# A diffusion transformer layer: when up's seeds are copied, which memory the first modulated tokens take, and where the second token tile's transposes stand

## The chip, the cores and the metric

The kernel runs on one core of a Trainium2 chip. The metric is the device time of one execution in microseconds, the median of several runs. A core has a matrix engine (TensorE, PE in the profile, with its weight loads as PEld), a vector engine (VectorE, DVE), a scalar engine (ScalarE, ACT), GpSimd (POOL) and SyncE (SP), which issues most transfers. Each engine works through its own instructions in the order in which they were written out; between engines there are only semaphores. Matrix results go to eight banks of accumulation memory (PSUM), each 128 x 512 numbers; everything else lies in the core's main memory (SBUF), where a buffer that is given to a new use must first be done with the old one.

## The reference

One layer over 256 latent tokens of width 2048 and 256 context tokens. The conditioning vector gives shifts, scales and gates; the tokens are modulated, attended and projected, normalised, modulated again and sent through a gated feed-forward block of hidden width 5632, and normalised once more. What matters here is the middle of this:

```python
sh1, sc1, g1, sh2, sc2, g2 = ada_mods(c, w_ada[layer], b_ada[layer])
...
x = layer_norm(DN_ALPHA * x + g1 * (heads @ w_out[layer]), ln1_g[layer], ln1_b[layer])
x = layer_norm(DN_ALPHA * x + g2 * swiglu(modulate(x, sh2, sc2), w_gate[layer], w_up[layer], w_down[layer]),
               ln2_g[layer], ln2_b[layer])
```

with `modulate(x, shift, scale) = x * (1 + scale) + shift` and `swiglu(u) = (silu(u @ w_gate) * (u @ w_up)) @ w_down`.

## The kernel before

**Products.** Float32 products are made of three passes: a number is split into a high part that the matrix engine takes (`hi`, an ACT cast, L330) and a remainder (`lo`, a DVE subtraction, L331), and `mm3` adds hi·hi (L340), lo·hi (L341) and hi·lo (L342). The tokens are split likewise into `u2h` and `u2l`. A loaded piece of weights is 512 columns by two groups of 128 rows; it serves both token tiles (t = 0, 1; 128 tokens each), so that one piece carries twelve passes of 512 columns.

**The transition into the feed-forward block.** The first token tile is normalised, and its columns 0 to 3 (groups of 128) are transposed by `z_flip(0, kk)` (L1444) into two banks. Meanwhile PE forms the conditioning vector's sums (`m1_sums`, L1413; PE multiplies the loaded conditioning weights there). `z_rest(t, kk)` modulates two columns with ACT (L1651), casts them into `u2h` (L1653) and DVE subtracts the remainder into `u2l` (L1654). Its working tile `uf2` comes from the pool `pb`, tag `t2k`, which begins where the earlier phase's buffers lay. `first_products(i, t, js)` then multiplies these columns by the first pieces of w_gate (i = 0) and w_up (i = 1). For the second tile, `scalars(1)` (a chain of small DVE instructions that ends with L1227, the normalised columns), `z_flip(1, kk)`, `second_shifts` (small matmuls L1426, DVE L1429) and `z_rest(1, kk)` follow. The conditioning sums of DVE (L465) are put between by the tile scheduler, which orders the instructions after this region by their data; up to the region's end (`region.__exit__`) the order is that of the code. A later `z_part(kk)` does the same as `z_flip` and `z_rest` for both tiles at once (L1471, L1476, L1478, L1479).

**The feed-forward block.** Ten of the eleven blocks of 512 hidden columns are done in five pairs f0 = 0, 2, 4, 6, 8. In a pair, `folded` forms one quarter of w_gate's contraction with seven products in place of eight: sums and differences of weight pieces (DVE L1535, L1538, L1539, L1545, L1547) and ACT copies from bank to bank (L1534, L1542, L1550) stand between the products. Between these, `up` multiplies the pieces of w_up into two banks of the `wk` pool. From the second pair on these banks start from an earlier partial sum kept in main memory (`spill`): ACT copies it into the banks (L1724, the seeds), and after the last piece ACT copies the sum back (L1730); in the first pair DVE adds (L1732). Then the gate's remaining pieces follow, and `gated_half` adds gate's earlier part (DVE L1558) and takes Silu (ACT L1559). DVE multiplies by up (L1599), and the result is turned by a DVE transposition (L1569) and a trip through DRAM (SP, L1574 and L1579). At a pair's start the code of the next pair begins only after the Silu of the last gate.

**Small things.** `grp`, a table for a later reduction of the conditioning vector, is formed by DVE at its first use (L1149), and `onesr` by an ACT cast (L1767) whose place the scheduler picks.

Of the kernel before, what the change touches and what calls it, by code (L numbers as in the profile page):

```python
# [265 lines left out]
def dit_layer(ctx: ExitStack, tc: tile.TileContext, x, c, cx, c_ctx, w_ada, b_ada, w_in, q_norm_g,  # L266
# [876 lines left out]
    grp = []  # L1143

    def folded_columns(sb, n):

        if not grp:
            grp.append(pb.tile([P, 32], F32, tag="grp", name="grp"))
            nc.vector.reduce_sum(grp[0], ident.rearrange("p (a i) -> p i a", a=4), axis=AX.X)  # L1149
        r = pb.tile([P, 32], F32, tag="fold", name="fold")  # L1150
        for h in range(0, n, 4):
            t = pb.tile([P, NB], F32, tag="t2k", name="flip", bufs=4)
            nc.vector.transpose(t, sb[:, h * P : (h + 4) * P])
            nc.vector.reduce_sum(r[:, 4 * h : 4 * h + 16], t.rearrange("p (b r) -> p b r", r=32), axis=AX.X)
# [307 lines left out]
    u2h = pb.tile([P, KD, SEQ], F32R, tag="u2h", name="u2h")  # L1462
    u2l = pb.tile([P, KD, SEQ], F32R, tag="u2l", name="u2l")
    hTh = [pb.tile([P, 4, SEQ], F32R, tag=f"hTh{f}", name="hTh") if f < KF // 4 - SPLIT_F else None for f in range(KF // 4)]
    hTl = [pb.tile([P, 4, SEQ], F32R, tag=f"hTl{f}", name="hTl") if f < KF // 4 - SPLIT_F else None for f in range(KF // 4)]
# [179 lines left out]
    def z_rest(t, kk):  # L1645

        ps = zbanks[t, kk]
        tt = slice(t * P, (t + 1) * P)
        uf = pb.tile([P, 2, SEQ], F32, tag="t2k", name="uf2", bufs=4)[:, :, :P]
        for j in range(2):  # L1650
# [52 lines left out]
    def turn():  # L1703
# [3 lines left out]
        for e in [e for e in flips if e[0] <= 0]:  # L1707
            flips.remove(e)
            e[1]()

    for f0 in range(0, SPLIT_F, 2):
        for f in (f0, f0 + 1):
            if 5 <= f < 9:
                residual_base(f - 5)
        ups = {}

        def up(i, g):
            f = f0 + i
            su = [spills[f][1][:, t, :] for t in range(NT)]
            if g == groups[f]:  # L1720
                ups[i] = [wk_bank() for _ in range(NT)]
                for t in range(NT):
                    if f0:
                        nc.scalar.copy(ups[i][t], su[t])  # L1724
            project(ups[i], w_up, f, g, groups[f] * 4, KD - 1, f0 > 0)
            turn()
            if g == ng - 1:
                for t in range(NT):
                    if f0:
                        nc.scalar.copy(su[t], ups[i][t])  # L1730
                    else:
                        nc.vector.tensor_add(su[t], su[t], ups[i][t])  # L1732

# [31 lines left out]
    g2sb = pb.tile([P, D], F32, tag="u2h", name="g2sb")  # L1765
    onesr = pb.tile([P, P], F32R, tag="onesr", name="onesr")
    nc.scalar.copy(onesr, ones)  # L1767
    def l2_loads():
# [151 lines left out]
```

## Time and profile before

| what | value |
|---|---|
| runs of the kernel | 1128.13, 1130.04, 1130.06 us; median 1130.04 us |
| the profiled execution | 1130.85 us, of which the span of the instructions is 1129.1 us |
| mean granted clock of the matrix engine in it | 0.996 of full speed |
| DVE busy | 880.7 us, 78% of the span, 1105 instructions |
| ACT busy | 589.1 us, 52% of the span, 859 instructions |
| data read from and written to DRAM | 304.07 MB and 16.25 MB |

The profile is read from the outside in: the share of busy time says which engine can be the bound, the waits say what that engine stood still for, and the timeline around such a wait says which instruction came last there. In a timeline row stand the start and the duration in us, the engine, the line and operation, what is written from what, how many instructions the row joins, and in brackets how long the engine had stood idle before and what ended that.

### The profile page before, as it was taken

To read this page: it belongs to the slowest core of one execution; us is meant where nothing else is said; L and a number is where in the kernel's file an instruction comes from. 1 tells how busy PE (TensorE), PEld (TensorE's weight loads), DVE (VectorE), ACT (ScalarE), POOL (GpSimd) and SP (SyncE) were. 2 spreads that over 40 slices of the span, in tenths; PEclk is the share of its full clock that TensorE was granted. 3 is DMA by queue.
4 is the path that set the end of the run, shared out by engine and by line. 5 is a ranking of instruction groups with operands and counts; after the bars stand their busy time and mean duration, and the time that the engine had idled before them with its cause. 6 is when DMAs were issued, how large, how long until landed. Compare 5 with 4: busy or idle time off the path is not lost.

```text
span 1129.1 us, 14104 instructions
## 1 busy us (share of the span) xinstructions
PE 1104.7 (98%) x5225; PEld 884.8 (78%) x5225; DVE 880.7 (78%) x1105; ACT 589.1 (52%) x859; POOL 35.1 (3%) x82
## 2 busy tenths in 40 slices
PE   8999999999999999999999999999999999999996
PEld 6766688777887687888888878888788888888884
DVE  5763589899999798777778786988976788676576
ACT  3341554878685255444465565766754344343442
POOL 1000030110100000000000000000000000000000
PEclk9999999999999999999999999999999999999998
DMA  9999999778999769898956767778788798887542
GB/s 322 390 382 375 389 362 372 248 237 282 342 325 386 254 260 312 302 349 310 335 174 219 249 194 254 235 246 265 225 273 276 274 373 297 305 318 259 191 147 75
DMA packets 178318, 321.26 MB, mean 285 GB/s; under 512 B 8733, under 2 KB 43197, under 8 KB 175944
## 3 DMA queue, kind: packets, MB, share of 16 engines
q1 hardware_dynamic: 177528, 320.03, 81.1%
q8 instruction: 41, 0.67, 0.2%
q10 hardware_dynamic: 720, 0.33, 0.1%
q14 instruction: 29, 0.23, 0.1%
HBM read 304.07 MB, written 16.25 MB: 284 GB/s over the span
## 4 chain that ended last, share of the span: by engine, by line
PE 86%; DMA 6%; DVE 3%; ACT 3%; SPq 1%; issue 1%; ACTq 0%; DVEq 0%
PE acc L340 22%; PE acc L342 22%; PE acc L341 22%; PE wk L340 5%; PE wk L342 5%; PE wk L341 5%; DMA raw<-in_w_in_dram 3%; PE wk L1080 2%; PE wk L653 1%; DVE lo L331 1%; DMA raw<-in_w_out_dram 1%; DMA lgb<-in_ln_g_dram 1%; DMA spill<-hd 1%; DMA pd<-hx 1%; SPq L568 1%
## 5 line engine op out<-in xcount | busy, mean ns | idle before, releaser
L330 ACT CAST hi<-raw 128x1024 fp32r<-128x1024 f32 x273 | 284.7, 1054 | 272.2 <-PE acc L342 212.3
L331 DVE TENSOR_TENSOR lo<-raw,hi 128x1024 fp32r<-128x1024 f32 x273 | 328.9, 1219 | 117.6 <-ACT hi L330 113.4
L340 PE MATMUL acc<-hi,u2h 128*128 128x512 f32 x422 | 165.0, 391 | 2.0 <-ACT u2h L1653 1.5
L341 PE MATMUL acc<-lo,u2h 128*128 128x512 f32 x422 | 164.3, 389 | 0.0
L342 PE MATMUL acc<-hi,u2l 128*128 128x512 f32 x422 | 164.1, 390 | 0.0
L602 ACT CAST hi<-raw 128x1024 fp32r<-128x1024 f32 (+1 forms) x86 | 87.4, 1030 | 116.1 <-DMA raw<-in_w_in_dram 64.2
L465 DVE SCALAR_TENSOR_TENSOR adav<-raw,cs,adav 128x512 f32<-128x512 f32 (+1 forms) x128 | 121.2, 947 | 19.2 <-DMA raw<-in_w_ada_dram 17.2
L340 PE MATMUL acc<-hi,hTh 128*128 128x512 f32 x344 | 133.5, 389 | 0.4 <-ACT acc L1845 0.4
L342 PE MATMUL acc<-hi,hTl 128*128 128x512 f32 x344 | 133.7, 389 | 0.0
L341 PE MATMUL acc<-lo,hTh 128*128 128x512 f32 x344 | 133.7, 389 | 0.0
L605 DVE TENSOR_TENSOR lo<-raw,hi 128x1024 fp32r<-128x1024 f32 (+1 forms) x86 | 101.3, 1194 | 16.9 <-ACT hi L602 16.4
L340 PE MATMUL acc<-hi,uh 128*128 128x512 f32 x256 | 103.8, 405 | 1.7 <-ACT uh L768 0.8
L341 PE MATMUL acc<-lo,uh 128*128 128x512 f32 x256 | 100.6, 393 | 0.6 <-DVE lo L605 0.5
L342 PE MATMUL acc<-hi,ul 128*128 128x512 f32 x256 | 100.1, 391 | 0.4 <-DVE ul L783 0.4
L340 PEld LDWEIGHTS acc<-hi,u2h 128*128 128x128 f32 x422 | 79.1, 188 | 19.4 <-ACT u2h L1653 2.4
L340 PE MATMUL wk<-hi,u2h 128*128 128x512 f32 x232 | 90.5, 390 | 2.9 <-ACT wk L1724 2.9
L342 PEld LDWEIGHTS acc<-hi,u2l 128*128 128x128 f32 x422 | 79.2, 188 | 17.3 <-DVE u2l L1654 0.6
L341 PEld LDWEIGHTS acc<-lo,u2h 128*128 128x128 f32 x422 | 79.2, 188 | 16.2
L342 PE MATMUL wk<-hi,u2l 128*128 128x512 f32 x232 | 90.3, 389 | 0.0
L341 PE MATMUL wk<-lo,u2h 128*128 128x512 f32 x232 | 90.3, 389 | 0.0
L340 PEld LDWEIGHTS acc<-hi,hTh 128*128 128x128 f32 x344 | 64.6, 188 | 14.1 <-ACT acc L1845 0.8
L342 PEld LDWEIGHTS acc<-hi,hTl 128*128 128x128 f32 x344 | 64.6, 188 | 13.5
(262 smaller groups left out, 1552.3 us busy)
## 6 DMA issues: line engine op xcount, KB each, us to landing
raw<-in_w_ada_dram SPq DMA_DIRECT2D x70, 1024.0 KB, 7.9
raw<-in_w_gate_dram SPq DMA_DIRECT2D x44, 1024.0 KB, 6.5
raw<-in_w_up_dram SPq DMA_DIRECT2D x44, 1024.0 KB, 6.3
raw<-in_w_down_dram SPq DMA_DIRECT2D x44, 1024.0 KB, 5.3
raw<-in_w_ada_dram SPq DMA_DIRECT2D x48, 512.0 KB, 6.8
raw<-in_w_in_dram SPq DMA_DIRECT2D x18, 1024.0 KB
raw<-in_w_out_dram SPq DMA_DIRECT2D x16, 1024.0 KB, 4.9
pd<-hx SPq DMA_DIRECT2D x64, 128.0 KB, 5.0
```

What stands on the lines that cost most here:

```text
L330: nc.scalar.copy(hi[:, :n], raw[:, s : s + n])
L331: nc.vector.tensor_tensor(lo[:, :n], raw[:, s : s + n], hi[:, :n].bitcast(F32), op=ALU.subtract)
L340: nc.tensor.matmul(ps, lhsT=xh, rhs=w[0], start=first, stop=False, skip_group_check=seeded)
L341: nc.tensor.matmul(ps, lhsT=xh, rhs=w[1], start=False, stop=False, skip_group_check=seeded)
L342: nc.tensor.matmul(ps, lhsT=xl, rhs=w[0], start=False, stop=last, skip_group_check=seeded)
L465: nc.vector.scalar_tensor_tensor(a[:, c : c + piece], raw[:, f : f + piece], cs[:, 4 * (g * (G4 * NB // w) + j) + 2, None], a[:, c : c + p ...
L568: nc.sync.dma_start(room.t, w[k0 * P : (k0 + 1) * P, c0 : c0 + width])
L602: nc.scalar.copy(hl.hi[:, :n], raw.t[:, s : s + n])
L605: nc.vector.tensor_tensor(hl.lo[:, :n], raw.t[:, s : s + n], hl.hi[:, :n].bitcast(F32), op=ALU.subtract)
L653: nc.tensor.matmul(bank.t[32 * j : 32 * j + 32, :width], lhsT=cs[:, 4 * k + 2 - 2 * i : 4 * k + 34 - 2 * i], rhs=raw.t[:, c * width : (c + ...
L1080: nc.tensor.matmul(o_ps.t[:, : 2 * P].rearrange("p (g q) -> p g q", q=32), lhsT=v, rhs=pv[:, k], start=k == 0, stop=k == 3)
```

## The change

Four things are altered.

1. The four `uf2` tiles of `z_rest` are allocated at once, directly behind `u2h` and `u2l` (`rests`), so that they lie in other memory than before; what is allocated from `pb` after them moves along by 8 KB per partition.
2. `first_products(1, 0, ...)` multiplies three columns ahead of `z_flip(1, kk)` in place of two, and one after it in place of two. The copy of the conditioning sum (`adav1`) follows behind.
3. `grp` and `onesr` are formed at the region's end.
4. Up's seeds are copied by a function `seeds(f)`. `up` calls it where its block has no banks yet; for the first block of the next pair it is called ahead of the gate's last pieces and Silu of the second block of the pair before.

```diff
+    def group_sums():
+        grp.append(pb.tile([P, 32], F32, tag="grp", name="grp"))
+        nc.vector.reduce_sum(grp[0], ident.rearrange("p (a i) -> p i a", a=4), axis=AX.X)
+
     def folded_columns(sb, n):
 
-        if not grp:
-            grp.append(pb.tile([P, 32], F32, tag="grp", name="grp"))
-            nc.vector.reduce_sum(grp[0], ident.rearrange("p (a i) -> p i a", a=4), axis=AX.X)
...
+    rests = {(t, kk): pb.tile([P, 2, SEQ], F32, tag="t2k", name="uf2", bufs=4)[:, :, :P] for t in range(NT) for kk in (0, 2)}
...
-        uf = pb.tile([P, 2, SEQ], F32, tag="t2k", name="uf2", bufs=4)[:, :, :P]
+        uf = rests[t, kk]
...
     scalars(1)
+    first_products(0, 0)
+    first_products(1, 0, (0, 1, 2))
+    for kk in (0, 2):
+        z_flip(1, kk)
+    first_products(1, 0, (3,))
     adav1 = vector_sums(NB)
     nc.scalar.copy(adav1, bank1.t)
-    first_products(0, 0)
-    first_products(1, 0, (0, 1))
-    for kk in (0, 2):
-        z_flip(1, kk)
-    first_products(1, 0, (2, 3))
...
+    group_sums()
+    onesr = pb.tile([P, P], F32R, tag="onesr", name="onesr")
+    nc.scalar.copy(onesr, ones)
     region.__exit__(None, None, None)
...
+    ups = {}
+
+    def seeds(f):
+        ups[f] = [wk_bank() for _ in range(NT)]
+        for t in range(NT):
+            if f > 1:
+                nc.scalar.copy(ups[f][t], spills[f][1][:, t, :])
+
...
-        ups = {}
-
         def up(i, g):
             f = f0 + i
             su = [spills[f][1][:, t, :] for t in range(NT)]
-            if g == groups[f]:
-                ups[i] = [wk_bank() for _ in range(NT)]
-                for t in range(NT):
-                    if f0:
-                        nc.scalar.copy(ups[i][t], su[t])
-            project(ups[i], w_up, f, g, groups[f] * 4, KD - 1, f0 > 0)
+            if f not in ups:
+                seeds(f)
+            project(ups[f], w_up, f, g, groups[f] * 4, KD - 1, f0 > 0)
...
         for i, f in enumerate((f0, f0 + 1)):
+            if i and f + 1 < SPLIT_F:
+                seeds(f + 1)
             for g in range(groups[f], ng):
```

The changed code's lines stand one to eight lines lower (the seeds' copy is L1722, gate's sum and Silu L1560 and L1561). Three places show how the instructions move.

**The second token tile, ACT and DVE.** On ACT, with the semaphores waited for, the modulations of the first tile stood like this before (`uf_...` are the working tiles, `DMAHW` are transfers; the row L1767 is the cast of `onesr`):

```order
L1651 ACTIVATE uf_3724<-wk,mB,mA 128x128 [waits DMAHW2_49,DMAHW4_49,DMAHW1_49,DMAHW5_49,PE_49,Pool_49]
L1651 ACTIVATE uf_3724<-wk,mB,mA 128x128
L1767 CAST onesr<-ones 128x128 [waits DMAHW2_49,DMAHW1_49]
L1653 CAST u2h<-uf_3724 128x2x128 [waits Activation_49]
L1651 ACTIVATE uf_3729<-wk,mB,mA 128x128 x2
```

and now:

```order
L1653 ACTIVATE uf_3698<-wk,mB,mA 128x128 [waits PE_49,Pool_49]
L1653 ACTIVATE uf_3698<-wk,mB,mA 128x128
L1655 CAST u2h<-uf_3698 128x2x128 [waits Activation_49]
L1653 ACTIVATE uf_3699<-wk,mB,mA 128x128 [waits PE_49]
L1653 ACTIVATE uf_3699<-wk,mB,mA 128x128
L1655 CAST u2h<-uf_3699 128x2x128 [waits Activation_49]
```

The waits for transfers are gone, and the wait for PE is one for each of the two transposed banks: `uf_3698` no longer shares memory with the loaded conditioning weights, so that only the transposes and the modulation's coefficients (POOL) are waited for, where before the last `m1_sums` was the PE instruction that had to be over. On DVE, from the end of the second tile's `scalars(1)` on, the rows before were these (L465 are conditioning sums, L1429 `second_shifts`, L1654 the second tile's two remainders):

```order
L1227 TENSOR_SCALAR xt<-xt,mv,ly 128x512
L465 SCALAR_TENSOR_TENSOR adav<-raw,cs,adav 128x512 x3
L1429 TENSOR_TENSOR sh_147<-wk,bcol 128x8
L1654 TENSOR_TENSOR u2l<-uf_3788,u2h 128x2x128
L1654 TENSOR_TENSOR u2l<-uf_3793,u2h 128x2x128
L1227 TENSOR_SCALAR xt<-xt,mv,ly 128x512 x6
```

and now:

```order
L1228 TENSOR_SCALAR xt<-xt,mv,ly 128x512
L465 SCALAR_TENSOR_TENSOR adav<-raw,cs,adav 128x512 x2
L1430 TENSOR_TENSOR sh_147<-wk,bcol 128x8
L465 SCALAR_TENSOR_TENSOR adav<-raw,cs,adav 128x512
L1656 TENSOR_TENSOR u2l<-uf_3700,u2h 128x2x128
L465 SCALAR_TENSOR_TENSOR adav<-raw,cs,adav 128x512
L1656 TENSOR_TENSOR u2l<-uf_3701,u2h 128x2x128
```

A fourth sum has come ahead of the second remainder, and one sum now stands between the shifts and the first remainder.

**The next columns, PE.** `z_part(4)` and `z_part(6)` transpose eight squares of the normalised tokens (L1471, now L1473) in the middle of the first blocks' products. The products that read the new columns are those that wait for ACT for the second time. Before:

```order
L1471 MATMUL wk<-ident,xt 128x128 x8
L340 MATMUL acc<-hi,u2h 128x512 [waits Activation_49]
L340 MATMUL acc<-hi,u2h 128x512
L341 MATMUL acc<-lo,u2h 128x512 [waits DVE_49]
L342 MATMUL acc<-hi,u2l 128x512
L341 MATMUL acc<-lo,u2h 128x512
L340 MATMUL acc<-hi,u2h 128x512 [waits Activation_49]
```

and now:

```order
L1473 MATMUL wk<-ident,xt 128x128 x3
L340 MATMUL acc<-hi,u2h 128x512 [waits Activation_49]
L341 MATMUL acc<-lo,u2h 128x512 [waits DVE_49]
L342 MATMUL acc<-hi,u2l 128x512
L340 MATMUL acc<-hi,u2h 128x512
L341 MATMUL acc<-lo,u2h 128x512
L342 MATMUL acc<-hi,u2l 128x512
L340 MATMUL acc<-hi,u2h 128x512
L341 MATMUL acc<-lo,u2h 128x512
L342 MATMUL acc<-hi,u2l 128x512
L340 MATMUL acc<-hi,u2h 128x512
L340 MATMUL acc<-hi,u2h 128x512 [waits Activation_49]
```

Ten passes over older columns follow the transposes, where there were five. On ACT one weight cast (L330) that stood between the two casts of the new columns now stands ahead of their modulation.

**A pair's start, ACT and DVE.** On ACT the rows around the Silu of the first pair's last gate were, at the start of pair f0 = 2:

```order
L1559 ACTIVATE spill<-spill 128x512 x2
L330 CAST hi<-raw 128x1024 x3
L1724 COPY wk<-spill 128x512
L1559 ACTIVATE spill<-spill 128x512 x2
L1534 COPY acc<-wk 128x512
L1724 COPY wk<-spill 128x512
L330 CAST hi<-raw 128x1024 x4
```

and now:

```order
L1722 COPY wk<-spill 128x512
L330 CAST hi<-raw 128x1024 x5
L1561 ACT_TABLE_LOAD
L1561 ACTIVATE spill<-spill 128x512 x2
L330 CAST hi<-raw 128x1024 x4
L1561 ACTIVATE spill<-spill 128x512 x2
L1536 COPY acc<-wk 128x512
L330 CAST hi<-raw 128x1024 x3
```

Both seeds have gone up past the first Silu (the other one stands higher still), and a fourth cast stands ahead of the second. On DVE the order at the starts of pairs 4, 6 and 8 has changed with it; pair 8 before:

```order
L331 TENSOR_TENSOR lo<-raw,hi 128x1024
L1599 TENSOR_TENSOR spill<-spill 128x512
L1538 TENSOR_TENSOR raw<-raw 128x1024
L1569 STREAM_TRANSPOSE spill<-spill 128x4x4x32
L331 TENSOR_TENSOR lo<-raw,hi 128x1024 x2
L1539 TENSOR_TENSOR raw<-raw 128x1024
L331 TENSOR_TENSOR lo<-raw,hi 128x1024
```

and now:

```order
L331 TENSOR_TENSOR lo<-raw,hi 128x1024
L1601 TENSOR_TENSOR spill<-spill 128x512
L331 TENSOR_TENSOR lo<-raw,hi 128x1024
L1571 STREAM_TRANSPOSE spill<-spill 128x4x4x32
L1540 TENSOR_TENSOR raw<-raw 128x1024
L1541 TENSOR_TENSOR raw<-raw 128x1024
L331 TENSOR_TENSOR lo<-raw,hi 128x1024 x2
```

Both subtractions of `folded` (L1538 and L1539, now L1540 and L1541) now stand ahead of the remainder of up's second pair of pieces; before, one of them came behind it.

More of the change, by code (lines that the diff above doesn't have):

```diff
@@ L1729, in up @@
                     if f0:
-                        nc.scalar.copy(su[t], ups[i][t])
+                        nc.scalar.copy(su[t], ups[f][t])
                     else:
-                        nc.vector.tensor_add(su[t], su[t], ups[i][t])
+                        nc.vector.tensor_add(su[t], su[t], ups[f][t])
         def between(n):
@@ L1765, in dit_layer @@
     g2sb = pb.tile([P, D], F32, tag="u2h", name="g2sb")
-    onesr = pb.tile([P, P], F32R, tag="onesr", name="onesr")
-    nc.scalar.copy(onesr, ones)
     def l2_loads():
```

## The prediction

> **What bounds the kernel now.** First the page, for the engine that can be the bound, then the waits of that engine.
>
> ```profile
> span 1129.1 us, 14104 instructions
> PE 1104.7 (98%) x5225; PEld 884.8 (78%) x5225; DVE 880.7 (78%) x1105; ACT 589.1 (52%) x859; POOL 35.1 (3%) x82
> PE wk L340 <- ACT wk L1724: 2.9, 2, 2.3
> PE acc L340 <- ACT u2h L1653: 1.5, 1, 1.5
> PE acc L340 <- ACT u2h L1478: 0.5, 1, 0.5
> ```
>
> PE is busy for 98% of the span, so the time is PE's work, which the change leaves as it is, plus what PE stands still. The three waits (line, what ended the wait, us in total, times, longest) are those that the change reaches, 4.9 us in all; a fourth, for L1227, shows in the row of 398.31 below with 0.30. Nothing here can bring more than about that, and it is had only where the next thing PE needs is not late too. So I walk through each place in the timeline. Passes of 512 columns start 0.228 us apart, as the rows below show (394.42 to 397.62: 14 passes).
>
> **The transition.**
>
> ```profile
> 389.85 0.44 PE L1444 MATMUL wk<-ident,xt 128*128 128x128 f32 x2
> 390.22 1.92 PE L1413 MATMUL wk<-raw,cs 128*32 128x512 f32 x16
> 391.81 0.30 SPq L448 DMA_DIRECT2D adav<-in_b_ada_dram  x1
> 392.26 0.81 ACT L1651 ACTIVATE uf<-wk,mB,mA 128x128 f32<-128x128 f32 x2 [6.81 <-PE wk L1413]
> 393.14 0.41 ACT L1653 CAST u2h<-uf 128x256 fp32r<-128x256 f32 x1
> 393.61 0.50 PE L340 MATMUL acc<-hi,u2h 128*128 128x512 f32 x1 [1.47 <-ACT u2h L1653]
> 394.42 0.40 PE L340 MATMUL acc<-hi,u2h 128*128 128x512 f32 x1
> 397.62 0.39 PE L342 MATMUL acc<-hi,u2l 128*128 128x512 f32 x1
> 397.62 0.55 DVE L1227 TENSOR_SCALAR xt<-xt,mv,ly 128x512 f32<-128x512 f32 x1
> 398.08 2.32 DVE L465 SCALAR_TENSOR_TENSOR adav<-raw,cs,adav 128x512 f32<-128x512 f32 x3
> 398.31 0.63 PE L1444 MATMUL wk<-ident,xt 128*128 128x128 f32 x4 [0.30 <-DVE xt L1227]
> 398.69 0.47 PE L340 MATMUL acc<-hi,u2h 128*128 128x512 f32 x1
> 400.17 0.95 PE L1426 MATMUL wk<-sel,adav 128*128 128x4 f32 x8
> 401.15 0.17 DVE L1429 TENSOR_TENSOR sh<-wk,bcol 128x8 f32<-128x8 f32 x1 [0.76 <-PE wk L1426]
> 401.24 0.75 DVE L1654 TENSOR_TENSOR u2l<-uf,u2h 128x256 fp32r<-128x256 f32 x2
> 401.71 0.50 PE L342 MATMUL acc<-hi,u2l 128*128 128x512 f32 x1
> 404.67 1.21 DVE L331 TENSOR_TENSOR lo<-raw,hi 128x1024 fp32r<-128x1024 f32 x1
> ```
>
> ACT's first modulation waited for the last L1413, though its banks were transposed by 390.3. With other memory the two modulations (0.81) and casts (0.41) of both column pairs are over by about 391.6, while PE is still at L1413 to 392.14. PE's first product then starts at about 392.2 in place of 393.61. In the new order 21 passes follow: 392.2 + 0.34 for the first + 20 x 0.228 = 397.1. The transposes take 0.38 (398.31 to 398.69): 397.5. Their DVE chain starts about 2.5 us earlier, after the earlier remainder, and ends near 395.1, so this wait goes. Three passes (0.78, with a restart) and L1426 (0.81 to the next product) give 399.1, and the first L342 on the second tile could come 0.54 later at 399.6, where it stood at 401.71.
>
> There DVE is late next. It works two sums, then L1429, which waits for L1426 until about 399.2 and takes 0.17, a third sum (2.32/3 = 0.77) and the first remainder (0.38): 400.5. The L342 starts at 400.55: **1.16 us gained** of 2.1. The bounds: 2.1 if the sums weren't in the way; 0.7 if the sums can't start before 398.08, where they start now and where I can't see since when their data was there (two to 399.6, L1429, third sum, remainder to 400.95). I take 1.16, since the bias row that the first sum adds to (L448) was asked for at 391.81, 6.3 us before 398.08. The next need is the first gate remainder (L331, 404.67 + 1.21 = 405.88). On DVE `grp` (0.36) now stands ahead of it and the six normalisations start earlier, so it ends where it did; PE comes to it at about 405.95. That margin is nothing: up to 0.2 may go there.
>
> **The next columns.**
>
> ```profile
> 434.42 1.03 PE L1471 MATMUL wk<-ident,xt 128*128 128x128 f32 x8
> 436.22 0.40 PE L341 MATMUL acc<-lo,u2h 128*128 128x512 f32 x1
> 436.48 0.62 ACT L1478 CAST u2h<-uf 128x512 fp32r<-128x512 f32 x1
> 437.15 0.50 PE L340 MATMUL acc<-hi,u2h 128*128 128x512 f32 x1 [0.53 <-ACT u2h L1478]
> 437.45 1.05 ACT L330 CAST hi<-raw 128x1024 fp32r<-128x1024 f32 x1
> ```
>
> PE should have started a pass at 436.45 and started at 437.15: 0.70 lost. Now ten passes in place of five stand ahead of this product, so PE reaches it 1.14 later, at about 437.6. The weight cast that stood behind (1.05, less the idle time of ACT that it fills) now stands ahead of the modulation and puts the cast's end from 437.1 to about 437.5. **0.70 gained**, with a bound of 0.5 if the cast is 0.1 to 0.2 later than that.
>
> **The seeds, pair 2.**
>
> ```profile
> 651.81 1.27 DVE L1558 TENSOR_TENSOR spill<-spill,acc 128x512 f32<-128x512 f32 x2
> 652.09 0.39 PE L342 MATMUL wk<-hi,u2l 128*128 128x512 f32 x1
> 652.52 1.23 ACT L1559 ACTIVATE spill<-spill 128x512 f32<-128x512 f32 x2 [3.85 <-DVE spill L1558]
> 653.00 1.22 DVE L1538 TENSOR_TENSOR raw<-raw 128x1024 f32<-128x1024 f32 x1
> 654.17 0.58 ACT L1724 COPY wk<-spill 128x512 f32<-128x512 f32 x1
> 654.80 0.50 PE L340 MATMUL wk<-hi,u2h 128*128 128x512 f32 x1 [2.32 <-ACT wk L1724]
> ```
>
> The second seed stands behind two Silu and a bank copy, and these wait 3.85 us for DVE. The pass due at 652.32 starts at 654.80: 2.48 lost. With the seed copied long before, PE goes on. Next late could be DVE, which doesn't get faster: behind L1538 (653.00, 1.14 to the next) come L1599 (0.60) and the remainder of the third piece (1.13), ready at 655.9; PE, 24 passes after 650.96, needs it at about 656.65. Following DVE on to the pair's next remainders I find margins of 0.5 to 1.5 us everywhere, so **2.48 gained**; below, 1.7 if DVE runs 1.2 us behind this count.
>
> The Trainium skill, in "PSUM — Partial Sum Buffer", section "Engine vs sequencer instructions", says that ScalarE's queue is strictly first in, first out; the row of 654.17 agrees, since a copy whose data had long been there waited behind a Silu. By that rule a seed that is moved up takes whatever it waits for with it, which speaks against the change and is the second rival.
>
> **The seeds, pairs 4, 6 and 8.**
>
> ```profile
> 791.02 1.10 ACT L1724 COPY wk<-spill 128x512 f32<-128x512 f32 x2
> 791.65 0.50 PE L340 MATMUL wk<-hi,u2h 128*128 128x512 f32 x1 [0.56 <-ACT wk L1724]
> 792.72 0.69 DVE L1599 TENSOR_TENSOR spill<-spill 128x512 f32<-128x512 f32 x1 [0.16 <-ACT spill L1559]
> 793.33 1.22 DVE L1538 TENSOR_TENSOR raw<-raw 128x1024 f32<-128x1024 f32 x1
> 795.09 2.32 DVE L331 TENSOR_TENSOR lo<-raw,hi 128x1024 fp32r<-128x1024 f32 x2
> 797.33 1.22 DVE L1539 TENSOR_TENSOR raw<-raw 128x1024 f32<-128x1024 f32 x1
> ```
>
> Pairs 4 and 6 have no wait for a seed. At pair 8 the product due at 790.93 started at 791.65: 0.72 lost, and saved. But here the new DVE order costs: L1599 still starts near 792.7 (a weight cast on ACT takes the time of the seeds), then a remainder (1.14), the transposition (0.63), L1538 and L1539 (1.14 each) and the remainder that up's second pair of pieces needs (1.18), together with L1599's 0.61 ready at 798.5. PE, 30 passes and two more after 790.93, wants it at 798.2. A stall of 0.3 to 0.5 is new: **0.27 gained** net. The same order at pairs 4 and 6 leaves, by the same count, margins of 0.3 to 0.5 and 0.85 us: nothing gained or lost.
>
> What else moves (`grp`, `onesr`, `adav1`'s copy) is under 0.7 us on engines that wait there, and I cost it at nothing; without that cover it would be 0.3 for each cast or reduction.
>
> **The sum.** 1.16 + 0.70 + 2.48 + 0.27 = 4.6 us off the profiled execution's 1130.85, of which 1.75 lie around the span: 1126.25. That execution is 0.8 above the median of 1130.04, so the forecast on that scale is **1125.5 us**. The most, with nothing given back, is 2.1 + 0.70 + 2.48 + 0.72 = 6.0: 1124.0. The least by the bounds above is 0.7 - 0.2 + 0.5 + 1.7 + 0 = 2.7: 1127.3.
>
> **The rivals.** First: DVE takes the gain back at the pairs' starts. For it: L1538 and L1539 now stand together ahead of a remainder at three starts, and the margins are small. Against it: that DVE has idle time between the starts and begins each of them fresh. If DVE runs 1.0 us later than I count, the starts lose 0.4 at pair 2, 0.6 at pair 4, 0.15 at pair 6 and 1.0 more at pair 8: 2.2 of the 4.6, so 1127.6.
>
> Second, slower: the moved seeds hold up ACT. ACT works in order, and casts stand behind each of the eight seeds that moved. A seed waits for its bank; if it waits as long as the longest wait above, 3.85 us, the weight cast behind it is late by that less ACT's usual idle time ahead of a cast:
>
> ```profile
> 630.76 1.05 ACT L330 CAST hi<-raw 128x1024 fp32r<-128x1024 f32 x1 [1.66 <-PE acc L342]
> ```
>
> So it costs from a wait of 1.66 on, 2.2 us each. One of the two in each of four pairs would cost 8.8, and 1130.0 - 4.6 + 8.8 = 1134.2. Against it: in the new order a seed waits for a bank's copy or sum that ends where ACT now idles.
>
> Third: the seed of pair 2 doesn't come earlier after all, because its bank isn't free until the last products: then 2.48 stays, 1128.0. Against it: the order shows the copies ahead of the first Silu, and nothing of the last gate in what they wait for.
>
> **How the numbers follow.** My forecast with its own range, 1124.0 to 1126.6, has a chance of 0.60; the first rival, 1126.6 to 1128.6, 0.24; the third 0.08; the second 0.05; still faster than 1124.0, 0.03. A measurement of this kernel can tell about 0.2% or 2.3 us, so faster means under 1127.8. Faster: 0.60 + 0.03 + half of the first rival (0.13) + a little of the third (0.02) = 0.78; slower 0.05; within 0.2% the rest, 0.17. The range goes from 1123.5, half a microsecond of scatter under the most, to 1128.5, which takes in the first and the third rival.
>
> **What would show it.** Right: no wait of PE for L1653's successor above 0.1 us, the first product near 392.2, a wait for u2l or for DVE of up to 0.9 near 400, no wait for a seed at pair 2, a wait for lo near 0.4 at pair 8. Wrong: a PE wait for lo above 0.5 us at the starts of pairs 4 or 6, an ACT wait at a seed of more than 1.6 us, or a product at 394 still.

## The result, and the profile after

| what | before | changed |
|---|---|---|
| median of 7 runs each, us | 1129.85 (1126.93 to 1130.32) | 1124.39 (1123.15 to 1127.95) |
| profiled execution, us | 1130.85 | 1124.52 |
| its span, us | 1129.1 | 1122.7 |

The changed kernel takes 0.996 of the time of the kernel before, with an interval from 0.9945 to 0.9975. That is 5.5 us between the medians, with bounds of 2.8 and 6.2 us. The forecast was 1125.5, and the time lies inside its range. How much of that was insight and how much the luck of one profiled execution is what the experiments are about.

First the page of the changed kernel, and of PE's waits (line, what ended the wait, us in total, times, longest) all that end behind the transition.

```profile
span 1122.7 us, 14106 instructions
PE 1104.0 (98%) x5225; PEld 886.7 (79%) x5225; DVE 880.7 (78%) x1105; ACT 589.9 (53%) x859; POOL 36.4 (3%) x82
PE acc L342 <- DVE u2l L1656: 0.7, 1, 0.7
PE acc L340 <- ACT acc L1853: 0.4, 1, 0.4
```

PE's busy time is what it was (1104.0 beside 1104.7). Of the waits that the change reaches, the four of before are gone and one is new, for u2l; the wait for L1853 stood in the profile of before too (there it is L1845). So the whole gain is standstill taken away, and it can be added up place by place.

The transition in the changed kernel's timeline:

```profile
387.85 0.81 ACT L1653 ACTIVATE uf<-wk,mB,mA 128x128 f32<-128x128 f32 x2 [3.57 <-PE wk L1445]
389.04 1.92 PE L1414 MATMUL wk<-raw,cs 128*32 128x512 f32 x16
390.89 0.50 PE L340 MATMUL acc<-hi,u2h 128*128 128x512 f32 x1
...
395.28 1.54 DVE L465 SCALAR_TENSOR_TENSOR adav<-raw,cs,adav 128x512 f32<-128x512 f32 x2 [1.44 <-DMA adav<-in_b_ada_dram]
395.79 0.60 PE L1445 MATMUL wk<-ident,xt 128*128 128x128 f32 x4
396.93 0.95 PE L1427 MATMUL wk<-sel,adav 128*128 128x4 f32 x8
397.91 0.17 DVE L1430 TENSOR_TENSOR sh<-wk,bcol 128x8 f32<-128x8 f32 x1 [1.10 <-PE wk L1427]
398.00 0.75 DVE L465 SCALAR_TENSOR_TENSOR adav<-raw,cs,adav 128x512 f32<-128x512 f32 x1
398.66 0.42 DVE L1656 TENSOR_TENSOR u2l<-uf,u2h 128x256 fp32r<-128x256 f32 x1
399.13 0.50 PE L342 MATMUL acc<-hi,u2l 128*128 128x512 f32 x1 [0.68 <-DVE u2l L1656]
```

ACT's modulation is now released by the transposes (L1445) and runs beside L1414, so the first product stands right behind the conditioning sums, 1.85 us after the start of the last L1414 row, where it stood 3.39 us after it (390.22 to 393.61). What is late next is DVE, as forecast: its conditioning sum stands between the shifts and the remainder. Counted from the same PE row, because both executions share all code up to there, the first L342 on the second tile came after 11.49 us and comes after 10.09 (399.13 - 389.04): 1.40 us gained.

The next columns (L1473 transposes them, and the cast L1480 releases their product):

```profile
431.93 1.04 PE L1473 MATMUL wk<-ident,xt 128*128 128x128 f32 x8
432.72 0.48 PE L340 MATMUL acc<-hi,u2h 128*128 128x512 f32 x1
434.44 0.62 ACT L1480 CAST u2h<-uf 128x512 fp32r<-128x512 f32 x1
434.89 0.73 PE L340 MATMUL acc<-hi,u2h 128*128 128x512 f32 x2
```

From 432.72 to 434.89 PE runs without a gap: nine passes, 0.31 apart behind the transposes and then 0.23, and the row of two L340 at 434.89 joins the tenth and the first product on the new columns, 0.70 us gained.

The seeds: how the view of one line shows all sixteen copies (start of the first and the last, then how long ACT stood idle before one, and until when; who waited for them is an empty list):

```profile
L1722 ACT COPY wk<-spill x16: 582/591/603, 605.5 to 798.4; 128x512 f32<-128x512 f32 x16
  DVE spill L1547: 1.1, 1
who waited for it (us, times):
```

The first seed is copied at 605.5, where the first stood at 648.1 before. The one that PE waited for at pair 2 is the second; it is copied at 624.42, and PE comes to its bank at 649.11, twelve passes after the pair's first product into `wk`, as before:

```profile
624.42 0.58 ACT L1722 COPY wk<-spill 128x512 f32<-128x512 f32 x1
649.11 0.39 PE L340 MATMUL wk<-hi,u2h 128*128 128x512 f32 x1
```

PE waits for none; between these two executions 2.48 us are gained at pair 2 and 0.72 at pair 8. Pair 8's start, where the forecast expected a new stall:

```profile
782.94 1.24 ACT L336 CAST hTh<-spill 128x512 fp32r<-128x512 f32 x2 [0.57 <-DMA spill<-hd]
790.88 2.35 DVE L331 TENSOR_TENSOR lo<-raw,hi 128x1024 fp32r<-128x1024 f32 x2
791.95 0.62 PE L340 MATMUL wk<-hi,u2h 128*128 128x512 f32 x2
792.41 0.39 PE L341 MATMUL wk<-lo,u2h 128*128 128x512 f32 x1
```

The first of the two remainders is ready at about 792.06 (790.88 plus half of 2.35), and PE wants it at 792.41: a margin of 0.35 us, and no stall.

The sum in these two executions is 1.40 + 0.70 + 2.48 + 0.72 = 5.30. From the last L1414 row to the end the kernel before took 738.88 us (1129.1 - 390.22) and the changed one takes 733.66 (1122.7 - 389.04): 5.22 us. The other 1.2 us of the 6.4 between the spans lie ahead of that row, in code that the change doesn't touch: the row's start lay between 388.9 and 390.3 in all the profiles of this study, of either order. It is scatter and no part of the gain.

### The profile page after: what moved, and what is told of

The parts are those of the page before. It is cut to its first block, busy times and chain, and to the rows that moved or that the text cites. A ratio compares the mean times of both kernels' runs of the same rounds, so it can differ in the third digit from the quotient of the medians.

```text
span 1122.7 us, 14106 instructions
## 1 busy us (share of the span) xinstructions
PE 1104.0 (98%) x5225; PEld 886.7 (79%) x5225; DVE 880.7 (78%) x1105; ACT 589.9 (53%) x859; POOL 36.4 (3%) x82
## 4 chain that ended last, share of the span: by engine, by line
PE 94%; DMA 3%; ACT 1%; DVE 1%; issue 0%; ACTq 0%; SPq 0%; DVEq 0%
PE acc L340 24%; PE acc L342 23%; PE acc L341 23%; PE wk L340 6%; PE wk L342 6%; PE wk L341 5%; PE wk L1080 2%; DMA raw<-in_w_in_dram 2%; PE wk L653 2%; PE wk L754 1%; DMA xt<-in_x_dram 0%; PE wk L1414 0%; ACT hi L602 0%; PE wk L484 0%; PE wk L688 0%; PE wk L983 0%
## 5 line engine op out<-in xcount | busy, mean ns | idle before, releaser
L330 ACT CAST hi<-raw 128x1024 fp32r<-128x1024 f32 x273 | 285.8, 1055 | 279.8 <-PE acc L342 212.6
L340 PE MATMUL acc<-hi,u2h 128*128 128x512 f32 x422 | 165.0, 391 | 0.0
L342 PE MATMUL acc<-hi,u2l 128*128 128x512 f32 x422 | 164.2, 390 | 0.7 <-DVE u2l L1656 0.7
L341 PE MATMUL acc<-lo,u2h 128*128 128x512 f32 x422 | 164.3, 389 | 0.0
L340 PE MATMUL acc<-hi,hTh 128*128 128x512 f32 x344 | 133.5, 389 | 0.4 <-ACT acc L1853 0.4
L342 PE MATMUL acc<-hi,hTl 128*128 128x512 f32 x344 | 133.8, 389 | 0.0
L341 PE MATMUL acc<-lo,hTh 128*128 128x512 f32 x344 | 133.8, 389 | 0.0
L465 DVE SCALAR_TENSOR_TENSOR adav<-raw,cs,adav 128x512 f32<-128x512 f32 (+1 forms) x128 | 121.3, 947 | 13.7 <-DMA raw<-in_w_ada_dram 10.5
L340 PE MATMUL acc<-hi,uh 128*128 128x512 f32 x256 | 103.8, 405 | 2.1 <-ACT uh L768 0.8
L341 PE MATMUL acc<-lo,uh 128*128 128x512 f32 x256 | 100.5, 393 | 0.4 <-DVE lo L605 0.4
L342 PE MATMUL acc<-hi,ul 128*128 128x512 f32 x256 | 100.1, 391 | 0.4 <-DVE ul L783 0.4
L342 PEld LDWEIGHTS acc<-hi,u2l 128*128 128x128 f32 x422 | 79.2, 188 | 17.6 <-DVE u2l L1656 1.1
L340 PEld LDWEIGHTS acc<-hi,u2h 128*128 128x128 f32 x422 | 79.2, 188 | 17.3 <-ACT u2h L1655 0.8
L341 PEld LDWEIGHTS acc<-lo,u2h 128*128 128x128 f32 x422 | 79.2, 188 | 16.3
L341 PE MATMUL wk<-lo,u2h 128*128 128x512 f32 x232 | 90.3, 389 | 0.0
L342 PE MATMUL wk<-hi,u2l 128*128 128x512 f32 x232 | 90.3, 389 | 0.0
L340 PE MATMUL wk<-hi,u2h 128*128 128x512 f32 x232 | 89.8, 389 | 0.0
L340 PEld LDWEIGHTS acc<-hi,hTh 128*128 128x128 f32 x344 | 64.6, 188 | 14.3 <-ACT acc L1853 0.8
L342 PEld LDWEIGHTS acc<-hi,hTl 128*128 128x128 f32 x344 | 64.6, 188 | 13.5
```

Source lines behind the costliest of these rows:

```text
L330: nc.scalar.copy(hi[:, :n], raw[:, s : s + n])
L340: nc.tensor.matmul(ps, lhsT=xh, rhs=w[0], start=first, stop=False, skip_group_check=seeded)
L341: nc.tensor.matmul(ps, lhsT=xh, rhs=w[1], start=False, stop=False, skip_group_check=seeded)
L342: nc.tensor.matmul(ps, lhsT=xl, rhs=w[0], start=False, stop=last, skip_group_check=seeded)
L465: nc.vector.scalar_tensor_tensor(a[:, c : c + piece], raw[:, f : f + piece], cs[:, 4 * (g * (G4 * NB // w) + j) + 2, None], a[:, c : c + p ...
```

## The experiments

Each part of the change alone, and each taken away. The theory: the memory frees the transition, the later transposes free the next columns, the early seeds free pair 2, and DVE gives some back. The rivals: the memory alone does all of the transition and the rest is chance of the scheduler's order; or the seeds bring less than their stall shows, because DVE is late behind them. The first four kernels shared 29 runs of the kernel before, median 1128.96 us. The third part, `grp` and `onesr`, has no run of its own.

**The seeds alone** (part 4 on the kernel before).

```diff
+            if f not in ups:
+                seeds(f)
...
+            if i and f + 1 < SPLIT_F:
+                seeds(f + 1)
```

> The kernel before with the seeds part alone. If each wait is its own loss: the waits for L1724 (2.48 at pair 2, 0.72 at pair 8) go, the waits at 393.6, 398.3, 401.7 and 437.2 stay; 3.2 us faster than the kernel before, some 1126.6 us. If the seeds only pay because the transition starts the feed-forward block earlier, or if the vector engine takes the gain back at the pairs' starts: under 1.5 us faster, with waits for lo (L331) in their place.

Measured: 1127.04 us, a ratio of 0.9982 (0.9972 to 0.9991): 1.9 us, with bounds of 1.0 and 3.2. The waits of the transition and the next columns stay as before (1.47, 0.33, 0.53), no seed is waited for, and a wait for a remainder is new at pair 8. (Two more are small: PE loses 0.12 us at 656.43, in pair 2, and 0.09 at 671.64 to remainders that end 0.05 earlier.) From this kernel's timeline at pair 8:

```profile
783.14 1.05 ACT L330 CAST hi<-raw 128x1024 fp32r<-128x1024 f32 x1 [2.91 <-DMA raw<-in_w_up_dram]
784.76 1.29 DVE L1599 TENSOR_TENSOR spill<-spill 128x512 f32<-128x512 f32 x2 [0.93 <-ACT spill L1559]
795.22 2.36 DVE L331 TENSOR_TENSOR lo<-raw,hi 128x1024 fp32r<-128x1024 f32 x2
795.31 0.61 PE L340 MATMUL wk<-hi,u2h 128*128 128x512 f32 x2
796.50 0.50 PE L341 MATMUL wk<-lo,u2h 128*128 128x512 f32 x1 [0.57 <-DVE lo L331]
```

This is the stall that the prediction put there: two passes after 795.31, 0.46 later, PE wants the remainder, and it starts at 796.50, 0.74 lost. DVE had started its run of work late, behind a Silu that stood behind a weight cast, and this cast waited 2.91 us for its weights. From 784.76 to 796.50 DVE has no idle time, so that the delay arrives at PE undiminished.

**All but the seeds** (the changed kernel with part 4 taken back).

```diff
+            if g == groups[f]:
+                ups[i] = [wk_bank() for _ in range(NT)]
...
-            if i and f + 1 < SPLIT_F:
-                seeds(f + 1)
```

> The changed kernel with the seeds copied where they were before. If each wait is its own loss: the waits at the transition and at the next columns stay as in the changed kernel (a wait of about 0.7 for u2l, none for the next columns), and 2.48 and 0.72 come back at pairs 2 and 8; 3.2 us slower than the changed kernel, 2.1 us faster than before, some 1127.7 us. If the parts help each other: both differences come out otherwise by over 0.5 us in what the matrix engine stands still.

Measured: 1126.69 us, 0.9982 (0.9969 to 0.9996), 2.3 us. The transition and the next columns are those of the changed kernel (0.84 lost at u2l, nothing at the next columns). The seed's wait at pair 2 is back, but smaller than in the profile of before; it takes 1.74 us from PE, and at pair 8 0.29 us:

```profile
635.38 1.29 DVE L1491 SCALAR_TENSOR_TENSOR xt<-xt,lgb 128x512 f32<-128x512 f32 x2 [2.47 <-DMA lgb<-in_ln_g_dram]
651.18 0.50 PE L340 MATMUL wk<-hi,u2h 128*128 128x512 f32 x1 [1.59 <-ACT wk L1729]
```

**The transposes where they were** (the changed kernel with part 2 taken back).

```diff
+    adav1 = vector_sums(NB)
+    nc.scalar.copy(adav1, bank1.t)
     first_products(0, 0)
-    first_products(1, 0, (0, 1, 2))
+    first_products(1, 0, (0, 1))
     for kk in (0, 2):
         z_flip(1, kk)
-    first_products(1, 0, (3,))
-    adav1 = vector_sums(NB)
-    nc.scalar.copy(adav1, bank1.t)
+    first_products(1, 0, (2, 3))
```

> The changed kernel with the second part undone: two columns multiplied ahead of the second tile's transposes and two behind, adav1's copy in its old place; memory, tables and seeds stay changed. In its order one conditioning sum less stands ahead of the second tile's first remainder, and the ten passes at the next columns stay. If the sum ahead of the remainder is what the transition still waits for: the wait for u2l falls from 0.7 to under 0.15, and the kernel is 0.6 to 0.8 us faster than the changed one, some 1123.7 us. If the later transposes are needed to give the second tile's normalisation time: a wait for L1228 of 0.3 or more before the transposes comes back, and the time is the same or worse.

Measured: 1126.65 us, 0.9976 (0.9965 to 0.9988). The loss at u2l falls to 0.19, as expected. What I had expected of the next columns, that the ten passes stay, was wrong:

```profile
431.94 1.03 PE L1473 MATMUL wk<-ident,xt 128*128 128x128 f32 x8
434.67 0.50 PE L340 MATMUL acc<-hi,u2h 128*128 128x512 f32 x1 [1.70 <-ACT u2h L1480]
```

No pass at all stands between the transposes and the product that needs them. The scheduler puts 5 passes there in the kernel before, 10 in the changed one and none here, though this edit stands 35 us earlier in the program. Without the wait the product would have come 0.79 behind the transposes, as the pass at 432.72 does in the changed kernel, so that 1.94 us are lost (434.67 - 431.94 - 0.79). The position of the transposes alone doesn't decide this: in the kernel before and with part 4 or (below) part 1 alone they stand at the same position, and five passes follow. So part 3, or the parts together, takes the five away; no run tells which. At the second tile this kernel's first L342 comes 9.44 us after the last L1414 row (399.19 - 389.75). At pair 8 it waits for a remainder as well: 0.46 lost.

**The memory alone** (part 1 on the kernel before).

```diff
+    rests = {(t, kk): pb.tile([P, 2, SEQ], F32, tag="t2k", name="uf2", bufs=4)[:, :, :P] for t in range(NT) for kk in (0, 2)}
...
-        uf = pb.tile([P, 2, SEQ], F32, tag="t2k", name="uf2", bufs=4)[:, :, :P]
+        uf = rests[t, kk]
```

> The kernel before with the first part alone, the working tiles in other memory. If the shared memory was the cause of the late start: the modulation starts right behind the first transposes, the first product right behind the last L1413, the wait of 1.47 goes, and since the vector engine's chain then ends before the transposes their wait of 0.30 goes too; 1.7 to 2.0 us less at the transition, the 0.70 at the next columns and the seeds' 2.48 and 0.72 stay; some 1128.0 us. If the late start had another cause (the modulation's coefficients or the transposes): no change at 393.6.

Measured: 1126.86 us, 0.9984 (0.9972 to 0.9995). One allocation takes the transition's wait away:

```profile
390.05 1.93 PE L1413 MATMUL wk<-raw,cs 128*32 128x512 f32 x16
391.91 0.50 PE L340 MATMUL acc<-hi,u2h 128*128 128x512 f32 x1
```

The first product comes 1.86 us after the row's start, as in the changed kernel, and the first L342 of the second tile 9.44 us after it (399.49), 2.05 earlier than before and 0.65 earlier than in the changed kernel. It is the same 9.44 as in the kernel above, which has the parts 3 and 4 besides, so that these bring nothing at this place. The next columns lose 0.69, pair 2 1.68 and pair 8 nothing.

Each of the next four kernels has a single run, beside a single one of the kernel before at 1127.99 us; what counts in them is what PE loses at each place, not the time.

**The transposes later, alone** (part 2 on the kernel before).

```diff
+    first_products(0, 0)
+    first_products(1, 0, (0, 1, 2))
+    for kk in (0, 2):
+        z_flip(1, kk)
+    first_products(1, 0, (3,))
     adav1 = vector_sums(NB)
     nc.scalar.copy(adav1, bank1.t)
-    first_products(0, 0)
-    first_products(1, 0, (0, 1))
-    for kk in (0, 2):
-        z_flip(1, kk)
-    first_products(1, 0, (2, 3))
```

> The kernel before with the second part alone, the transposes later; memory, tables and seeds as before. If the second part is what gives the ten passes at the next columns: no wait at 437 (0.70 less), the first product still at about 393.6 behind the shared memory, no wait for L1227, and a wait for u2l of 0.2 to 0.9. If the next columns gain by the earlier start of the block: the 0.53 wait for L1478 stays.

Measured: 1127.45 us. The wait of 1.47 for ACT stays, the one for the normalised columns goes, u2l costs 0.84 in its place, and the next columns lose nothing. Pair 2 loses 1.75.

**The transposes earlier** (the changed kernel with one column of products ahead of them).

```diff
-    first_products(1, 0, (0, 1, 2))
+    first_products(1, 0, (0,))
     for kk in (0, 2):
         z_flip(1, kk)
-    first_products(1, 0, (3,))
+    first_products(1, 0, (1, 2, 3))
```

> The changed kernel with one column multiplied ahead of the second tile's transposes and three behind. The second tile's remainders then stand directly behind the shifts in the order, and at the next columns five passes stand as in the kernel before. If the order decides: no wait for u2l above 0.2, but the 0.5 to 0.7 at the next columns back; within 0.3 us of the changed kernel. If the next columns wait on something else: no wait there, and 0.7 us faster.

Measured: 1125.48 us. The loss at u2l is 0.19; five passes stand at the next columns again, and 0.69 is lost there:

```profile
432.96 0.71 PE L340 MATMUL acc<-hi,u2h 128*128 128x512 f32 x2
433.51 0.40 PE L341 MATMUL acc<-lo,u2h 128*128 128x512 f32 x1
433.75 0.40 PE L342 MATMUL acc<-hi,u2l 128*128 128x512 f32 x1
433.98 0.39 PE L341 MATMUL acc<-lo,u2h 128*128 128x512 f32 x1
434.90 0.50 PE L340 MATMUL acc<-hi,u2h 128*128 128x512 f32 x1 [0.53 <-ACT u2h L1480]
```

From the last L1414 row to the end it takes 733.7 us, as the changed kernel does. So what the later transposes gain at the next columns (0.70) they give back at u2l (0.65).

**Early seeds at pair 2 only.**

```diff
-            if i and f + 1 < SPLIT_F:
+            if i and f + 1 == 2:
```

> The changed kernel with the early seeds at pair 2 alone; at pairs 4, 6 and 8 they are copied where they were. If the vector engine's new order at pairs 4, 6 and 8 comes from the early seeds: the old order there, a wait of 0.5 to 0.7 for the seed at pair 8, none at 4 and 6; 0.7 us slower than the changed kernel. If it has another cause: the wait at pair 8 is gone here too, and the time is that of the changed kernel.

Measured: 1125.33 us. DVE's order at pair 8 is that of before, and PE waits there neither for a seed nor for a remainder. From the last L1414 row to the end: 733.6 us, as with all the early seeds. In this execution those of pairs 4, 6 and 8 would have brought nothing.

**More work for DVE** (the changed kernel with two additions of 512 columns more in each pair, whose result is not used).

```diff
+    junk = pb.tile([P, NB], F32, tag="junk", name="junk")
...
         tt(b12, b22, b12, op=ALU.subtract)
+        for _ in range(2):
+            tt(junk, b12[:, :NB], b12[:, NB:half], op=ALU.add)
```

> The changed kernel with two more additions of 128x512 (0.6 us each on the vector engine, their result is not used) behind the first subtraction of each pair's start, one ahead of each of up's next two remainders. In the changed kernel's profile these remainders are ready 0.37, 0.16 and 0.34 us before they are needed at pairs 4, 6 and 8. If that is the margin: waits for lo of 0.2 to 0.5 us with the first, and about as much again with the second, at each of the three pairs, 1.5 to 3 us in all. If the margin is larger than it looks (the remainders have another 1 us to go): no waits and the same time.

Measured: 1125.97 us. PE loses only 0.08 to 0.09 us to the first remainder at each of the three starts, and nothing to the second. But the order isn't the same: the scheduler put a folded product (709.16, 751.57 and 794.00, L340 on `fh`) between the two L340 and the L341 that reads the remainder, so that PE comes to it a pass later. Without this pass, by an estimate, 0.31 would have been lost (0.08 + 0.23) to an addition that takes 0.60, which would put the margin near 0.3. The margin at a fixed order wasn't measured.

The remaining three kernels stand beside 14 runs of the kernel before, median 1128.07 us.

**The changed kernel again**, without an edit.

> The changed kernel once more, unaltered, on the chip of the next two. If the wait for lo at pair 8 depends on when weights arrive in the single execution: this profile shows a wait of up to 0.6 there, or a margin other than 0.35; if it is fixed by the order: again none, with a margin of 0.3 to 0.4. The wait for u2l of 0.7 is the same either way. Some 0.995 to 0.997 of the kernel before.

Measured: 1125.28 us (1124.03 to 1127.17, 8 runs), 0.9976 (0.9965 to 0.9986): 2.8 us, with bounds of 1.6 and 3.9. Its only wait of the changed places is again the one for u2l (0.85 lost). At pair 8 the remainder is ready 0.38 us before PE needs it, where it was 0.35 in the first profile, and from the last L1414 row to the end it takes 733.57 us.

**The kernel before again**, one run, for whether its stalls are always the same.

> The kernel before once more, unaltered. Where the changed parts leave the seeds alone the wait for them at pair 2 was 1.5 to 1.6, in the profile of before 2.32, and at pair 8 0 to 0.3 in place of 0.56. If these sizes depend on when transfers land in the single execution: other sizes here too. If the parts of the change make them smaller: again 2.2 to 2.4 and 0.5 to 0.6.

Measured: 1127.89 us. The transition (1.47, 0.31) and the next columns (0.54) wait as they did. Pair 2 loses 1.34 in place of 2.48, and pair 8 loses nothing in place of 0.72:

```profile
636.92 1.29 DVE L1489 SCALAR_TENSOR_TENSOR xt<-xt,lgb 128x512 f32<-128x512 f32 x2 [2.05 <-DMA lgb<-in_ln_g_dram]
652.74 0.50 PE L340 MATMUL wk<-hi,u2h 128*128 128x512 f32 x1 [1.17 <-ACT wk L1724]
```

and in the profile from which the prediction was made:

```profile
638.99 1.29 DVE L1489 SCALAR_TENSOR_TENSOR xt<-xt,lgb 128x512 f32<-128x512 f32 x2 [3.21 <-DMA lgb<-in_ln_g_dram]
```

From this DVE row to PE's late product it is 15.82 us here (652.74 - 636.92) and 15.81 there (654.80 - 638.99), and 15.80 in the three kernels above whose seeds stand where they did: all but the seeds, the memory alone, the transposes alone. DVE works without idle time between the row and the sum that the Silu waits for. So the stall at pair 2 is the time at which the layer norm's row (`lgb`) lands plus 15.8, less the time at which PE is there. That is a reading of five profiles with one constant; a kernel in which the row lands earlier wasn't tried.

**The shifts behind the modulation**, in the changed kernel, to take the last new wait away.

```diff
-    second_shifts(adav1)
     for kk in (0, 2):
         z_rest(1, kk)
+    second_shifts(adav1)
```

> The changed kernel with the second tile's modulation written ahead of its shifts (z_rest(1, kk) before second_shifts). In the order the first remainder then no longer stands behind L1430, which waits for the matrix engine, though three sums are ahead of it; the ten passes at the next columns stay. If the remainder was late for standing behind L1430 and a sum: ready about 0.6 earlier, the wait for u2l falls from 0.7 to 0.1 or less, and the kernel is 0.6 to 0.8 us faster than the changed one. If the sums alone make it late, because they start only when their bias row has arrived: the wait falls by less than 0.3.

Measured: 1125.01 us, 0.9971 (0.996 to 0.9982), beside 0.9976 (0.9965 to 0.9986) of the changed kernel on the same chip: no difference can be told. In its timeline:

```profile
395.62 2.33 DVE L465 SCALAR_TENSOR_TENSOR adav<-raw,cs,adav 128x512 f32<-128x512 f32 x3 [1.12 <-DMA adav<-in_b_ada_dram]
398.14 0.43 DVE L1656 TENSOR_TENSOR u2l<-uf,u2h 128x256 fp32r<-128x256 f32 x1 [0.19 <-ACT u2h L1655]
398.95 0.40 PE L342 MATMUL acc<-hi,u2l 128*128 128x512 f32 x1
...
792.76 0.50 PE L341 MATMUL wk<-lo,u2h 128*128 128x512 f32 x1 [0.54 <-DVE lo L331]
```

The remainder now stands ahead of the fourth sum, the wait for u2l is gone, and the first L342 comes 9.26 us after the last L1414 row (398.95 - 389.69), 0.83 earlier than in the changed kernel; the next columns lose nothing. But pair 8 lost 0.70 to a late remainder in this execution, and the time to the end is that of the changed kernel (733.61). There ACT stood idle for 2.11 us until a transfer of `spill` through DRAM landed (0.57 in the changed kernel's profile).

## Why the prediction was right, and where it wasn't

**What bounds it: right.** PE's work stayed the same, and the gain is the standstill taken away at the four places named, no more.

**The transition: right in kind, 0.24 too small.** The first product comes behind L1414, DVE is late next, and the conditioning sums don't wait until 398.08: they start when their bias row lands (395.28, 1.44 us of idle time before). The term of 1.16 measured 1.40 because PE was at L1427 earlier than I counted (396.93 - 389.04 = 7.89 after the last L1414 row; by the prediction's own times, 398.3 - 390.22 = 8.1), and the shifts with it. What I did not see is that part 2 works against part 1 here: the memory alone brings 2.05 at this place.

**The next columns: right.** 0.70 forecast, 0.70 measured, by ten passes in place of five. But this gain hangs on an order that the scheduler finds: with the transposes one column ahead five passes stood there, and with the transposes two columns ahead none in one kernel and five in three others.

**Pair 2: the mechanism right, the size that of one execution.** The seed's wait goes wherever the seeds are early, and DVE is late behind it by 0.12 at the most (in the kernel with the seeds alone, where the row landed at 639.41). But 2.48 was the largest of five stalls: 1.34, 1.68, 1.74, 1.75 and 2.48, on the average 1.80 (8.99 / 5). My bound of 1.7 came from DVE's pace and not from this, and is above the smallest. In these five profiles the stall is what the row takes from its request (L1486) to its use, 7.00 to 8.15 us, less 5.66 to 5.69. In the changed kernel's first profile the row took 5.69 (627.73 to 633.42), so that by this estimate the old seeds would have cost next to nothing there. Over the twelve profiles without additions on DVE it took 5.7 to 8.8, on the average 7.2, which makes the typical gain an estimated 1.6.

**Pairs 4 and 6: right**, with margins of 0.37 and 0.16 in the changed kernel's profile (the first piece's remainder at the start, from its end to PE's use), thinner than the 0.85 counted for pair 6.

**Pair 8: the failed step.** The prediction said: "A stall of 0.3 to 0.5 is new: 0.27 gained net." In the changed kernel's two profiles there is no such stall, so that 0.72 was gained in the first: the remainder is ready 0.35 us early, and not 0.3 late. The term that was off is the start of L1599 (now L1601). It was taken from the profile of before, where ACT had just waited 1.75 us for `spill`, and stood 5.5 us ahead of PE's use of the remainder (798.2 - 792.7); in the changed kernel's first profile it stands 6.13 ahead (792.41 - 786.28), after a wait of 0.57. But neither is fixed. The seed's stall was 0.72, 0.29, 0, 0 and 0 in the five profiles with the old seeds, and 0 with the early seeds at pair 2 alone; the remainder's was 0.74, 0.46 and 0.70 in three kernels with all seeds early and 0 in three runs (the changed kernel twice, the earlier transposes). A margin of a few tenths lies there in either order, and late transfers go with the stalls. These rows of ACT, two of the kernel before, one of the transposes where they were and one of the shifts behind the modulation, stand ahead of three of them; the last row is L1601 in the changed kernel:

```profile
785.00 1.06 ACT L330 CAST hi<-raw 128x1024 fp32r<-128x1024 f32 x1 [2.34 <-DMA raw<-in_w_up_dram]
789.91 1.21 ACT L336 CAST hTh<-spill 128x512 fp32r<-128x512 f32 x2 [1.75 <-DMA spill<-hd]
786.02 1.22 ACT L336 CAST hTh<-spill 128x512 fp32r<-128x512 f32 x2 [1.87 <-DMA spill<-hd]
784.20 1.17 ACT L336 CAST hTh<-spill 128x512 fp32r<-128x512 f32 x2 [2.11 <-DMA spill<-hd]
786.28 0.68 DVE L1601 TENSOR_TENSOR spill<-spill 128x512 f32<-128x512 f32 x1
```

In the five executions that stalled at pair 8, ACT's longest wait for a transfer in the 20 us ahead was 1.87 to 2.91 us; in six of the seven others it was 0.26 to 0.60, and in one, the transposes earlier, 2.06 with a margin of 0.21 left. That transfers decide is read from this agreement; no kernel moved a landing alone, and neither profile of the changed kernel itself has a stall at pair 8. On the average the early seeds gain about 0.2 at pair 8 and lose about 0.3: nothing.

**The sum.** 4.6 was forecast, 5.3 is found between the two profiles, and the typical gain is smaller than both: 1.40 + 0.70 + 1.80 + 0 = 3.9 (3.7 with the 1.6). Between the second pair of profiles, from the last L1414 row, it is 3.3 (736.84 - 733.57). The two measurements with intervals, 2.8 to 6.2 and 1.6 to 3.9 us, overlap from 2.8 to 3.9. So the forecast's time came out close, with help from an execution of before that had both stalls at their largest.

**The rivals.** The first, DVE taking back, is real at pair 8, up to 0.74 us, and shows elsewhere with 0.12 at the most, less than the 2.2 it was priced at. The second didn't come: the one seed ahead of which ACT stood idle, for 1.1 us, is one that wasn't moved (at 662.41; 1.26 us in the profile of before), and 1.1 is below the 1.66 from which it would have cost. The Trainium skill's rule in "PSUM — Partial Sum Buffer", section "Engine vs sequencer instructions", that ScalarE's queue is first in, first out, is contradicted by no profile here. But a moved seed whose data are there holds up nothing: pair 2's two were copied 41 and 25 us before PE came to their banks. The third is refuted by the times of these two, 605.5 and 624.4.

## What to carry to other kernels

Where an engine waits for work that has no data in common with it, look at the memory: here one allocation in another place took nearly all of the transition's stall with it (2.05 of 2.1 us), while the reordering beside it gave back what it won. A stall read from one profile is one draw: before it enters a sum at full size, follow it back to what sets it, and if that is a transfer's landing (15.8 us ahead, in this case) take a second profile or a range. And where a scheduler orders the work, moving a piece shifts others that the diff doesn't touch (0, 5 or 10 passes, worth up to 2 us), so that parts of a change don't add up and are to be tried one by one.

## What the runs showed of the hardware that wasn't expected

The same transfer in the same program took different times: the layer norm's row was asked for at 630.84 and used at 638.99 in one execution of the kernel before, 8.2 us, and at 629.92 and 636.92 in another, 7.0 us; in the changed kernel's first profile it was 5.7 us (627.73 to 633.42). These are the rows, in this order:

```profile
630.84 0.46 SPq L1486 DMA_DIRECT2D lgb<-in_ln_g_dram  x1
629.92 0.46 SPq L1486 DMA_DIRECT2D lgb<-in_ln_g_dram  x1
627.73 0.46 SPq L1488 DMA_DIRECT2D lgb<-in_ln_g_dram  x1
633.42 1.29 DVE L1491 SCALAR_TENSOR_TENSOR xt<-xt,lgb 128x512 f32<-128x512 f32 x2 [0.79 <-DMA lgb<-in_ln_g_dram]
```

Since DVE has no idle time in the 12 us behind it, such a difference arrives at PE whole where the seeds stand as before: 8.15 less 7.00 is 1.15 us, and the stalls differ by 1.14 (2.48 less 1.34). The medians of the kernel before lay between 1127.99 and 1129.85 us in the four sets of 1, 7, 14 and 29 runs; whether that is the chips or such transfers stays open.
